# Staged first loads, other filler matmuls, and a planner that gives the shared port to whoever asked first: a two-layer hybrid trunk on one core

## The chip, the cores and the metric

The kernel runs on one core of one Trainium2 chip. The metric is the device time of one launch in microseconds (us), lower is better. Times of several runs are given by their median.

## The reference

A residual stream x of 512 tokens by 1024 channels passes two layers. In each layer a conditioning vector c gives shift, scale and gate; the normalized and modulated x is projected by one wide matrix, whose columns feed three causal token mixers (sparse attention over the top 128 keys, sliding-window attention with sinks, stick-breaking attention) and their gates; the merged result is projected back and added.

```python
for each layer:
    mod = silu(c) @ W_ada + b_ada             # shift, scale, gate
    u = rms_norm(x, g) * (1 + scale) + shift
    z = u @ W_in                              # all mixers, gates, merge gates
    y_b = mixer_b(z) * silu(gate_b)           # b = A, B, C
    merged = sum_b sigmoid(m_b) * (y_b @ W_br_b)
    x = x + gate * (merged @ W_out)
```

Everything is float32.

## The kernel before

**Matmuls.** x is held transposed, as 8 tiles of 128 channels by 512 tokens (k = 0 to 7; k = 0 to 3 in the tile `vc`, 4 to 7 in `va`). TensorE (PE) works on numbers rounded to a shorter form, so each weight chunk and each u is split into a high and a low part (`whi`, `wlo`, `uh`, `ul`), and each product is three matmuls: whi with uh, whi with ul, wlo with uh. A 256 KB chunk of weights is loaded into a tile `wstage` (four slots), cast to `whi`, and `wlo` is the difference of the two; the class `Chunks` (L632) loads and splits ahead of use.

**A recorded program.** No engine order is written by hand. The class `Recorder` (L244) notes every instruction with the engines that may run it, `price` (L304) gives it a modelled duration, and `forward` (L372) plans: it steps through the instructions, puts each at the earliest time that its engine, its inputs and its tile slots allow, and repeats this for five rounds, with the latest time that an instruction may start in one round (`latest`, L491) as its priority in the next. VectorE (DVE) and GpSimd (POOL) share a port in this model: of the instructions marked `port` only one runs at a time. For PE it also adds a cost when the shape of the matmul changes: modes are "c" (64 columns of the array, as in the mixers' products of probabilities and values), "t" (transposes) and "m" (all others). The best plan is emitted in order at L536, so every row of a profile has that line, and tiles are told apart by name. In the planner's loop the choice between engines is `if mine is not None and (best is None or mine < best[0])`, where `mine` is the triple of start time, priority and number: at equal start times the more urgent instruction goes.

**The start** (`start`, within `trunk`). Eight warm-up matmuls on ones, then silu(c) is broadcast over all partitions as `csr`. `norm(HALVES[0])` loads the first 256 tokens of x in four transfers, squares, sums and adds over partitions by a matmul with ones (`nones`), and makes 1/rms. `ada_load(j)` loads two tiles of 512 KB of the conditioning weights for channel tile j into slots called `Y` (five slots), and `ada_first(j)` (L706) makes shift and scale of that tile from each by one DVE scalar_tensor_tensor with csr, 128 by 1024, whose sum goes to `mods`, and `amul` from that. `make_u` (L755) turns x[k] into uh and ul by `mods` and `amul`. While PE has nothing to do, `ada_first` puts filler matmuls before the dot products: `FILL` (L42) says how many for each quarter of the weights, 11 in all, on the tiles `Y` as they land. `ch.load(1)` loads the two weight chunks of k = 0, `norm(HALVES[1])` the second half of x, and so on. All loads are issued by SyncE (SP) in one order and may start when their slot is free.

**What follows.** The first phase (`first_phase`, L893) takes seven output tiles over k = 0 to 7, k = 0 and 1 in halves of 256 tokens, then come the mixers, the merge gates and the output projection; the second layer repeats this without the start.

Of the kernel before, what the change touches and what calls it, by code (L numbers as in the profile page):

```python
# [32 lines left out]
S = 512  # L33
# [5 lines left out]
LOW = -3.0e38  # L39
TOPK = 128  # L40
WARM = 8
FILL = (2, 1, 4, 4, 0, 0, 0, 0)  # L42
BIG = 2.0 ** 100
SPACE = {"c0": 865, "c1": 7720, "c2": 1802, "a0": 1361, "a1": 13022, "a2": 500, "b0": 2448, "b1": 10119, "b2": 1676, "ag": 12129, "as": 6930, "t": 2422}
QCOST = 2408
# [198 lines left out]
class Recorder:  # L244
# [127 lines left out]
    def forward(self):  # L372
# [37 lines left out]
        while len(out) < len(self.list):  # L410
            best = None
            for name, e in E.items():
                free, pend, ready = e["free"], e["pend"], e["ready"]
                while pend and pend[0][0] <= free + 1e-9:
                    i = heapq.heappop(pend)[1]
                    ready[i] = self.list[i]
                mine = None
                for i in list(ready):
                    x = ready[i]
                    if x.taken:  # L420
                        del ready[i]
                        continue
                    y = x.alts[name]
                    at = max(free, port) if y.port else free
                    if len(x.alts) > 1 and self.elsewhere(x, name, at, E, port):
                        continue
                    key = (at, x.prio, i)
                    if mine is None or key < mine:
                        mine = key
                if mine is None or mine[0] > free + 1e-9:  # L430
                    while pend and self.list[pend[0][1]].taken:
                        heapq.heappop(pend)
                    if pend:
                        est, i = pend[0]
                        x = self.list[i]
                        at = max(est, port) if x.alts[name].port else est
                        key = (at, x.prio, i)
                        if (mine is None or key < mine) and not (len(x.alts) > 1 and self.elsewhere(x, name, at, E, port)):
                            mine = key
                        elif mine is None:  # L440
                            mine = None
                if mine is not None and (best is None or mine < best[0]):
                    best = (mine, name)
            assert best is not None, "no instruction may go"
            (at, _, i), name = best
            e, x = E[name], self.list[i]
            y = x.alts[name]
            x.taken, x.engine = True, name
# [1 line left out]
            hold = y.cost  # L450
            if name == "PE":
                if e["mode"] is not None and y.mode != e["mode"]:
                    hold += 0.18 if "c" in (y.mode, e["mode"]) else 0.08
                e["mode"] = y.mode
            x.start, x.hold = at, hold
            e["free"] = at + hold
# [102 lines left out]
def trunk(ctx, tc, xT, vecs, w_ss, w_gt, w_first, w_t, w_v, w_br, w_o, rope, consts, out):  # L559
# [68 lines left out]
    csr = fixed("csr", [P, D], F32)  # L628
    sk8 = fixed("sk8", [P, 8 * L], F32)


    class Chunks:  # L632
        LD, LS = LOAD_AHEAD, SPLIT_AHEAD
# [4 lines left out]
            self.used = set()  # L638
            self.nload = self.nsplit = 0

        def load(self, upto):
            while self.nload < min(upto + 1, len(self.seq)):
                i = self.nload
                if i >= 4 and i - 4 not in self.used:
                    break
                src, is_raw = self.seq[i][:2]
                n = src.shape[1]
                t = rec.tile("wstage", [P, S], F32)
                SP.dma_start(t[:, :n], src)
                self.raw[i] = (t, n)  # L650
                self.nload += 1
# [46 lines left out]
    def ada_ss(l, j, q):  # L698
        return op(0, lambda w: ada_step(l, j, q, w), (w_ss[l, j, q], True))

    def ada_load(j):
        st["wada", j] = [rec.tile("Y", [P, 2 * S], F32) for _ in range(2)]
        for i in range(2):
            SP.dma_start(st["wada", j][i].rearrange("p (a b) -> p a b", a=2), w_ss[0, j, 2 * i:2 * i + 2].rearrange("q p s -> p q s"))

    def ada_first(j):  # L706
        o = rec.tile("dot", [P, 4], F32)
        for i in range(2):
            w, m = st["wada", j][i], 8 * i + j
            if j < 2:  # L710
                for q in range(2):
                    for _ in range(FILL[4 * j + 2 * i + q]):
                        mm(st["nbank" if j else "warm"][:, :P], f(nones), w[:, S * q:S * q + P], not j)
            DVE.scalar_tensor_tensor(w, w, 1.0, csr, op0=OP.mult, op1=OP.mult, accum_out=o[:, i:i + 1])
            DVE.tensor_tensor(out=mods[0][:, m:m + 1], in0=o[:, i:i + 1], in1=b_ada[0][:, m:m + 1], op=OP.add)
        DVE.scalar_tensor_tensor(amul[0][:, j:j + 1], mods[0][:, 8 + j:9 + j], 1.0, g_sb[0][:, j:j + 1], op0=OP.add, op1=OP.mult)
# [665 lines left out]
    def start():  # L1382
# [17 lines left out]
        x = st["x"] = [xx[k // 4][:, k % 4] for k in range(KT)]  # L1400
        nb = st["nbank"] = st["rstd"] = sbank()

        def norm(cs_):
            for k in range(0, KT, 2):
                SP.dma_start(xx[k // 4][:, k % 4:k % 4 + 2, cs_], xT[:, k:k + 2, cs_])
            prev = None
            for k in range(0, KT, 2):
# [12 lines left out]
                prev = t  # L1420
            rstd_of(nb[:, cs_])

        norm(HALVES[0])
        for k in (0, 1):
            times_rstd(x[k], HALVES[0])
        ada_load(0)
        ada_first(0)
        ch.load(1)
        make_u(0, 0, x[0], HALVES[0])
        norm(HALVES[1])  # L1430
        for k in (0, 1):
            times_rstd(x[k], HALVES[1])
        ada_load(1)
        ada_first(1)
        make_u(0, 1, x[1], HALVES[0])
        make_u(0, 0, x[0], HALVES[1])
        make_u(0, 1, x[1], HALVES[1])
        ch.load(3)
        ada_load(2)

    sin_t = cos_t = tri0 = band = ident_b = cmask_b = None

# [110 lines left out]
```

## Time and profile before

| what | us |
|---|---|
| median of three runs | 1236.3 |
| the three runs | 1236.63, 1228.27, 1236.3 |
| the profiled execution | 1232.83 |
| its span in the trace | 1231.0 |
| PE busy in it | 1201.3 (98%) |
| DVE busy | 976.0 (79%) |
| ACT (ScalarE) busy | 559.5 (45%) |
| POOL busy | 258.2 (21%) |

The span runs from the first to the last instruction of the trace; the device time has 1.8 us around it. Busy time is what the engine spends in instructions other than waits and issues. In the profile PEld is the load of weights into the array, which runs beside the matmuls.

### The profile page before, as it was taken

How to read it: one execution, taken by the hardware profiler on the slowest of the kernel's cores; microseconds unless marked ns; L12 is line 12 of the kernel's file. 1: busy time of each engine (PE TensorE's matmuls, PEld its weight loads, DVE VectorE, ACT ScalarE, POOL GpSimd, SP SyncE). 2: the span in 40 equal slices, each digit the busy share in tenths (PEclk: the TensorE clock that was granted, in tenths of full speed). 3: DMA queues.
4: the chain of work that ended last, by engine and by line, in shares of the span. 5: the costliest groups of instructions: out<-in, count | busy, mean ns of one | idle time of the engine just before them, and what ended most of it. 6: DMA issues, size and time to landing. Idle time of an engine off the chain costs nothing.

```text
span 1231.0 us, 17835 instructions
## 1 busy us (share of the span) xinstructions
PE 1201.3 (98%) x5984; PEld 980.3 (80%) x5984; DVE 976.0 (79%) x2128; ACT 559.5 (45%) x1157; POOL 258.2 (21%) x278
## 2 busy tenths in 40 slices
PE   7999999999999999999999999999999999999997
PEld 6789777778878887778898987777787888877886
DVE  7966999999788887777475689999986888667654
ACT  4342678554256522642143258665533563244222
POOL 2210333433012211001211015253410111100120
PEclk8999999999999999999999999999999999999999
DMA  9644221324333455334533433223442333322343
GB/s 320 196 122 131 73 86 61 108 93 132 119 104 102 121 154 154 95 114 118 181 115 102 126 98 86 69 86 103 112 121 72 82 95 107 107 70 77 94 120 103
DMA packets 81915, 139.40 MB, mean 113 GB/s; under 512 B 10016, under 2 KB 22560, under 8 KB 81824
## 3 DMA queue, kind: packets, MB, share of 16 engines
q1 hardware_dynamic: 80672, 136.17, 37.8%
q10 hardware_dynamic: 1152, 2.10, 0.5%
q8 instruction: 47, 0.77, 0.3%
q14 instruction: 44, 0.36, 0.1%
HBM read 125.39 MB, written 4.19 MB: 105 GB/s over the span
## 4 chain that ended last, share of the span: by engine, by line
PE 79%; DVE 12%; ACT 3%; DMA 2%; issue 2%; SPq 1%; POOL 1%; DVEq 0%; ACTq 0%; POOLq 0%
PE ps_z L536 59%; PE ps_s L536 20%; DVE t L536 3%; ACT t L536 2%; DVE m L536 1%; DVE Q L536 1%; DVE score L536 1%; DMA wstage<-in_w_t 1%; DVE wstage L536 1%; SPq L536 1%; DVE Y L536 1%; DVE vc L536 1%; DVE e L536 1%; DMA vc<-in_xT 1%; DVE zc L536 0%
## 5 line engine op out<-in xcount | busy, mean ns | idle before, releaser
L536 PE MATMUL ps_z<-uh,whi 128*128 128x512 f32 (+1 forms) x908 | 357.8, 395 | 7.1 <-ACT uh L536 4.8
L536 PE MATMUL ps_z<-ul,whi 128*128 128x512 f32 (+1 forms) x908 | 356.8, 393 | 0.5 <-DVE ul L536 0.5
L536 PE MATMUL ps_z<-uh,wlo 128*128 128x512 f32 (+1 forms) x908 | 354.6, 391 | 0.9 <-DVE wlo L536 0.9
L536 POOL TENSOR_TENSOR wlo<-wstage,whi 128x512 fp32r<-128x512 f32 (+1 forms) x148 | 197.9, 1338 | 701.8 <-DVE whi L536 322.9
L536 PEld LDWEIGHTS ps_z<-uh,whi 128*128 128x128 f32 x908 | 170.3, 188 | 46.6 <-ACT uh L536 6.2
L536 PEld LDWEIGHTS ps_z<-ul,whi 128*128 128x128 f32 x908 | 171.0, 188 | 39.2 <-issue 3.3
L536 PEld LDWEIGHTS ps_z<-uh,wlo 128*128 128x128 f32 x908 | 170.5, 188 | 38.4 <-DVE wlo L536 1.6
L536 ACT CAST whi<-wstage 128x512 fp32r<-128x512 f32 (+2 forms) x153 | 90.8, 596 | 212.9 <-PE ps_z L536 147.5
L536 DVE CAST whi<-wstage 128x512 fp32r<-128x512 f32 (+2 forms) x169 | 69.8, 413 | 124.3 <-PE ps_z L536 104.9
L536 DVE TENSOR_TENSOR wlo<-wstage,whi 128x512 fp32r<-128x512 f32 (+2 forms) x224 | 147.3, 661 | 18.0 <-ACT whi L536 9.2
L536 PE MATMUL ps_z<-Y,whi 128*128 128x512 f32 x384 | 121.6, 396 | 0.2
L536 ACT ACTIVATE e<-ps_z 128x512 f32<-128x512 f32 x68 | 40.0, 592 | 121.7 <-PE ps_z L536 121.2
L536 PEld LDWEIGHTS ps_z<-Y,whi 128*128 128x128 f32 x384 | 71.6, 188 | 17.1 <-DVE xm L536 0.7
L536 ACT ACTIVATE e<-e 128x512 f32<-128x512 f32 x96 | 60.2, 631 | 40.4 <-DVE e L536 39.6
L536 PE MATMUL ps_z<-Y,wlo 128*128 128x512 f32 x192 | 76.0, 396 | 0.0
L536 ACT ACTIVATE t<-t 128x512 f32<-128x512 f32 x120 | 72.0, 627 | 5.5 <-DVE t L536 1.8
L536 ACT ACTIVATE t<-t,nm 128x256 f32<-128x256 f32 (+3 forms) x128 | 65.0, 510 | 18.5 <-DVE nm L536 18.5
L536 POOL CAST whi<-wstage 128x512 fp32r<-128x512 f32 (+1 forms) x50 | 31.4, 628 | 167.9 <-ACT vb L536 51.8
L536 PE MATMUL ps_s<-small,t 128*128 128x128 f32 x432 | 58.5, 275 | 4.6 <-ACT t L536 4.0
L536 PEld LDWEIGHTS ps_s<-small,t 128*128 128x128 f32 x432 | 49.7, 141 | 15.3 <-ACT t L536 7.3
L536 DVE SCALAR_TENSOR_TENSOR wstage<-wstage,csr 128x512 f32<-128x512 f32 x64 | 48.0, 751 | 10.6 <-DMA wstage<-in_w_ss 8.1
L536 DVE MAX8 m<-score 128x8 f32<-128x256 f32 (+2 forms) x96 | 53.3, 556 | 1.5
(201 smaller groups left out, 2080.3 us busy)
## 6 DMA issues: line engine op xcount, KB each, us to landing
wstage<-in_w_t SPq DMA_DIRECT2D x212, 256.0 KB, 2.7
wstage<-in_w_v SPq DMA_DIRECT2D x48, 182.0 KB, 2.4
Y<-in_w_ss SPq DMA_DIRECT2D x16, 512.0 KB, 6.4
m<-zs SPq DMA_DIRECT2D x128, 64.0 KB, 2.0
wstage<-in_w_gt SPq DMA_DIRECT2D x32, 256.0 KB, 2.6
wstage<-in_w_ss SPq DMA_DIRECT2D x32, 256.0 KB, 2.7
wstage<-in_w_o SPq DMA_DIRECT2D x32, 256.0 KB, 2.7
wstage<-in_w_first SPq DMA_DIRECT2D x16, 256.0 KB, 3.4
```

The lines of the kernel that those rows point to most:

```text
L536: getattr(self.real[engine], y.op)(*[real(a) for a in y.args], **{k: real(v) for k, v in y.kw.items()})
```

## The change

Three things are changed.

1. **Loads in stages.** `behind(t, v)` lets POOL copy one column of v into a tile t just before a load into t. The copy needs v's landing, and the load needs the copy, so the load is issued only after v has landed. It stands before the first two weight chunks (behind x's last piece of the first half), before the four pieces of x's second half (behind the first chunk), and before the conditioning weights of tiles 1 and 2 (behind the first and second chunk).
2. **Fillers.** The 11 matmuls on `Y` are gone; `busy` puts 24 in their place, 12 on the two first weight chunks and 12 on x[0] and x[1] after their scaling.
3. **The planner.** At equal start times the instruction goes that could have started first (`asked`: the later of its inputs' time and its engine's); priority decides only after that. A change of matmul shape is assumed to cost 0.095 us where the 64-column form is on either side (0.18 before), and nothing otherwise (0.08 before).

```diff
-FILL = (2, 1, 4, 4, 0, 0, 0, 0)
...
-                if mine is not None and (best is None or mine < best[0]):
-                    best = (mine, name)
+                if mine is not None:
+                    asked = max(free, self.list[mine[2]].est)
+                    if best is None or (mine[0], asked, mine) < best[:3]:
+                        best = (mine[0], asked, mine, name)
             assert best is not None, "no instruction may go"
-            (at, _, i), name = best
+            (at, _, i), name = best[2:]
...
-                    hold += 0.18 if "c" in (y.mode, e["mode"]) else 0.08
+                    hold += 0.095 if "c" in (y.mode, e["mode"]) else 0.0
...
+    def behind(t, v):
+
+        POOL.tensor_copy(out=t[:, 0:1], in_=v[:, 0:1])
+
...
-        def load(self, upto):
+        def load(self, upto, after=None):
...
                 t = rec.tile("wstage", [P, S], F32)
+                if after is not None:
+                    behind(t, after)
                 SP.dma_start(t[:, :n], src)
...
-            if j < 2:
-                for q in range(2):
-                    for _ in range(FILL[4 * j + 2 * i + q]):
-                        mm(st["nbank" if j else "warm"][:, :P], f(nones), w[:, S * q:S * q + P], not j)
             DVE.scalar_tensor_tensor(w, w, 1.0, csr, op0=OP.mult, op1=OP.mult, accum_out=o[:, i:i + 1])
...
+        def busy(n, v):
+            for _ in range(n):
+                mm(st["warm"][:, :P], f(nones), v[:, :P], True)
+
         norm(HALVES[0])
+        ada_load(0)
+        ch.load(1, x[6])
+        busy(6, ch.raw[0][0])
+        busy(6, ch.raw[1][0])
+        ada_first(0)
         for k in (0, 1):
             times_rstd(x[k], HALVES[0])
-        ada_load(0)
-        ada_first(0)
-        ch.load(1)
+            busy(6, x[k])
         make_u(0, 0, x[0], HALVES[0])
-        norm(HALVES[1])
+        norm(HALVES[1], ch.raw[0][0])
+        ada_load(1, ch.raw[0][0])
         for k in (0, 1):
             times_rstd(x[k], HALVES[1])
-        ada_load(1)
         ada_first(1)
...
         ch.load(3)
-        ada_load(2)
+        ada_load(2, ch.raw[1][0])
```

`norm` and `ada_load` take an `after` too and put `behind` before their loads in the same way.

**SP's order at the start.** `wstage` are weight chunks, `Y` conditioning weights, `vc` and `va` the halves of x; numbers tell tiles apart. Before, from the first Y on:

```order
L536 DMA Y_115<-in_w_ss 128x2x512
L536 DMA Y_118<-in_w_ss 128x2x512
L536 DMA wstage_122<-in_w_first 128x512
L536 DMA wstage_125<-in_w_first 128x384
L536 DMA Y_131<-in_w_ss 128x2x512
L536 DMA Y_136<-in_w_ss 128x2x512
L536 DMA wstage_140<-in_w_first 128x512
L536 DMA wstage_146<-in_w_first 128x384
L536 DMA vc_100<-in_xT 128x2x256
L536 DMA Y_151<-in_w_ss 128x2x512
L536 DMA va_108<-in_xT 128x2x256 x2
L536 DMA Y_179<-in_w_ss 128x2x512
```

The last piece of x's second half (vc_100) follows directly on these. Now, from the third Y-and-chunk pair on:

```order
L537 DMA wstage_122<-in_w_first 128x512
L537 DMA wstage_125<-in_w_first 128x384
L537 DMA wstage_145<-in_w_first 128x512
L537 DMA wstage_149<-in_w_first 128x384
L537 DMA vc_100<-in_xT 128x2x256
L537 DMA Y_184<-in_w_ss 128x2x512
L537 DMA va_108<-in_xT 128x2x256 x2
L537 DMA Y_182<-in_w_ss 128x2x512
L537 DMA Y_188<-in_w_ss 128x2x512
L537 DMA Y_195<-in_w_ss 128x2x512
L537 DMA Y_198<-in_w_ss 128x2x512
L537 DMA wstage_226<-in_w_first 128x512
```

Three more chunks and then the last piece of x's second half (vc_100) follow on these. The chunks of k = 0, gated behind x, are now wstage_145 and 149; those of k = 1 (122 and 125) are not gated and stand ahead of them. Y_182 and 188 belong to k = 1, Y_195 and 198 to k = 2, Y_184 to k = 3.

**DVE's order before u of k = 1.** uh1 is the high part of that u, `mods0` shift and scale, the rows with csr the dot products. Before:

```order
L536 SCALAR_TENSOR_TENSOR Y_136,dot_201<-Y_136,csr_70 128x1024
L536 TENSOR_TENSOR mods0_72<-dot_201,small_66 128x1
L536 TENSOR_TENSOR t_244<-t_244 128x256
L536 SCALAR_TENSOR_TENSOR amul0_74<-mods0_72,small_66 128x1
L536 SCALAR_TENSOR_TENSOR Y_151,dot_254<-Y_151,csr_70 128x1024
L536 TENSOR_TENSOR t_250<-t_250 128x256
L536 TENSOR_SCALAR uh1_261<-vc_100,amul0_74,mods0_72 128x256
```

Now:

```order
L537 SCALAR_TENSOR_TENSOR Y_182,dot_279<-Y_182,csr_70 128x1024
L537 TENSOR_TENSOR mods0_72<-dot_279,small_66 128x1
L537 SCALAR_TENSOR_TENSOR Y_188,dot_279<-Y_188,csr_70 128x1024
L537 TENSOR_TENSOR mods0_72<-dot_279,small_66 128x1
L537 SCALAR_TENSOR_TENSOR amul0_74<-mods0_72,small_66 128x1
L537 SCALAR_TENSOR_TENSOR Y_195,dot_293<-Y_195,csr_70 128x1024
L537 TENSOR_TENSOR mods0_72<-dot_293,small_66 128x1
L537 SCALAR_TENSOR_TENSOR Y_198,dot_293<-Y_198,csr_70 128x1024
L537 TENSOR_TENSOR mods0_72<-dot_293,small_66 128x1
L537 SCALAR_TENSOR_TENSOR amul0_74<-mods0_72,small_66 128x1
L537 SCALAR_TENSOR_TENSOR Y_184,dot_303<-Y_184,csr_70 128x1024
L537 TENSOR_SCALAR uh1_307<-vc_100,amul0_74,mods0_72 128x256
```

The dot products for k = 2 and the first of k = 3 now stand between those of k = 1 and its u.

**PE's order at mixer b of the first layer.** `t` are probabilities and `vb` values (64 columns of the array each), small,t are transposes, vc,Q the scores of another mixer. Before:

```order
L536 MATMUL ps_s<-t,vb 64x256 x3
L536 MATMUL ps_s<-t,vb 64x128
L536 MATMUL ps_s<-t,vb 64x256 x3
L536 MATMUL ps_s<-t,vb 64x128
L536 MATMUL ps_z<-ul_485,whi 128x512
```

Now:

```order
L537 MATMUL ps_s<-t,vb 64x256 x3
L537 MATMUL ps_s<-t,vb 64x128
L537 MATMUL ps_s<-vc,Q 128x256 x4
L537 MATMUL ps_z<-uh_211,whi 128x512
L537 MATMUL ps_z<-ul_224,whi 128x512
L537 MATMUL ps_s<-vc,Q 128x256
L537 MATMUL ps_s<-small,t 128x128 x7
L537 MATMUL ps_s<-vc,Q 128x256 x5
L537 MATMUL ps_s<-vc,Q 128x128 x2
L537 MATMUL ps_s<-t,vb 64x256 x3
L537 MATMUL ps_s<-t,vb 64x128
```

The two halves of the group, which stood together, are separated by 14 other rows' matmuls. Four of the eight groups of mixer b stand apart in this way, and two more of the groups of mixers a and c. Over the whole program 17 wlo subtractions move from POOL to DVE (10 of them into the two stretches in which DVE looks for the top 128 keys), and about a dozen whi casts from ACT to DVE.

## Rows read from the trace of the kernel before

**Rows 1.** The page, busy time of each engine (share of the span, instructions).

```profile
PE 1201.3 (98%) x5984; PEld 980.3 (80%) x5984; DVE 976.0 (79%) x2128; ACT 559.5 (45%) x1157; POOL 258.2 (21%) x278
```

**Rows 2.** Busy time by stretch: us and instructions, then TensorE's granted clock, DMA.

```profile
12.30:16.00 3.70, 0.02 (x1) 0.02 (x1) 3.63 (x9) 1.12 (x2) 0.71 (x1) 1.00 1.06 376
17.40:27.60 10.20, 7.85 (x30) 6.84 (x29) 8.25 (x21) 2.88 (x6) 1.74 (x1) 0.50 1.06 380
48.00:66.50 18.50, 16.71 (x71) 12.18 (x69) 16.57 (x34) 8.07 (x14) 3.76 (x5) 1.00 0.45 151
...
200.00:300.00 100.00, 95.42 (x465) 74.58 (x464) 95.34 (x218) 55.27 (x121) 40.69 (x40) 1.00 0.36 106
...
800.00:900.00 100.00, 95.78 (x465) 75.99 (x465) 95.47 (x219) 55.86 (x122) 41.56 (x41) 1.00 0.36 103
```

**Rows 3.** Timeline of ACT at the start: start, duration, what, [idle before <- releaser].

```profile
7.29 0.63 ACT L536 ACTIVATE t<-va 128x512 f32<-128x512 f32 x1 [0.57 <-DMA va<-in_xT]
...
11.39 0.51 ACT L536 CAST whi<-wstage 128x384 fp32r<-128x384 f32 x1 [0.28 <-DMA wstage<-in_w_first]
...
21.03 0.63 ACT L536 ACTIVATE t<-vc 128x512 f32<-128x512 f32 x1 [1.49 <-DMA vc<-in_xT]
```

**Rows 4.** Timeline of PE at the start (each 128-column filler counts as two).

```profile
10.21 2.05 PE L536 MATMUL ps_s<-Y,nones 128*128 128x128 f32 x16
15.98 0.50 PE L536 MATMUL ps_z<-uh,whi 128*128 128x256 f32 x2 [3.71 <-ACT uh L536]
...
16.79 0.28 PE L536 MATMUL ps_z<-uh,whi 128*128 128x256 f32 x1
16.91 0.28 PE L536 MATMUL ps_z<-ul,whi 128*128 128x256 f32 x1
...
21.42 0.79 PE L536 MATMUL ps_z<-uh,whi 128*128 128x256 f32 x2 [2.35 <-DVE uh L536]
```

**Rows 5.** The page, DMA issues: instructions, KB each, us from issue to landing.

```profile
wstage<-in_w_t SPq DMA_DIRECT2D x212, 256.0 KB, 2.7
```

**Rows 6.** Timeline of DVE and POOL, two dot products and the wlo beside one.

```profile
29.84 1.22 DVE L536 SCALAR_TENSOR_TENSOR Y<-Y,csr 128x1024 f32<-128x1024 f32 x1
...
31.60 1.31 POOL L536 TENSOR_TENSOR wlo<-wstage,whi 128x512 fp32r<-128x512 f32 x1 [12.46 <-PE ps_z L536]
...
31.66 2.33 DVE L536 SCALAR_TENSOR_TENSOR Y<-Y,csr 128x1024 f32<-128x1024 f32 x1
```

**Rows 7.** Timeline of PE, the first phase's last matmul.

```profile
65.32 0.39 PE L536 MATMUL ps_z<-uh,wlo 128*128 128x512 f32 x1
```

**Rows 8.** Timeline of PE, groups of mixer b, and the matmul behind one.

```profile
250.59 2.65 PE L536 MATMUL ps_s<-t,vb 128*64 128x256 f32 x16
253.16 0.50 PE L536 MATMUL ps_z<-ul,whi 128*128 128x512 f32 x1
...
345.99 0.65 PE L536 MATMUL ps_s<-t,vb 128*64 128x256 f32 x2
348.04 2.25 PE L536 MATMUL ps_s<-t,vb 128*64 128x256 f32 x14
...
370.16 2.25 PE L536 MATMUL ps_s<-t,vb 128*64 128x256 f32 x16
...
943.54 1.73 PE L536 MATMUL ps_s<-t,vb 128*64 128x256 f32 x8
```

**Rows 9.** The page, costliest groups: busy, mean ns, idle before, releaser.

```profile
L536 POOL TENSOR_TENSOR wlo<-wstage,whi 128x512 fp32r<-128x512 f32 (+1 forms) x148 | 197.9, 1338 | 701.8 <-DVE whi L536 322.9
...
L536 DVE TENSOR_TENSOR wlo<-wstage,whi 128x512 fp32r<-128x512 f32 (+2 forms) x224 | 147.3, 661 | 18.0 <-ACT whi L536 9.2
```

**Rows 10.** PE's waits from 100 to 1231 us: total, times, longest.

```profile
PE ps_s L536 <- ACT t L536: 4.0, 3, 2.0
PE ps_s L536 <- DVE Q L536: 3.4, 2, 1.7
...
PE ps_z L536 <- DVE wlo L536: 0.9, 2, 0.5
```

More of the change, by code (lines that the diff above doesn't have):

```diff
@@ L699, in ada_ss, with ada_load @@
         return op(0, lambda w: ada_step(l, j, q, w), (w_ss[l, j, q], True))
-    def ada_load(j):
+    def ada_load(j, after=None):
         st["wada", j] = [rec.tile("Y", [P, 2 * S], F32) for _ in range(2)]
         for i in range(2):
+            if after is not None:
+                behind(st["wada", j][i], after)
             SP.dma_start(st["wada", j][i].rearrange("p (a b) -> p a b", a=2), w_ss[0, j, 2 * i:2 * i + 2].rearrange("q p s -> p q s"))
@@ L1401, in start, with norm @@
         nb = st["nbank"] = st["rstd"] = sbank()
-        def norm(cs_):
+        def norm(cs_, after=None):
             for k in range(0, KT, 2):
+                if after is not None:
+                    behind(xx[k // 4][:, k % 4, cs_], after)
                 SP.dma_start(xx[k // 4][:, k % 4:k % 4 + 2, cs_], xT[:, k:k + 2, cs_])
```

## The prediction

> **What bounds the kernel now.** I read the shares first: TensorE (PE) is busy for 1201.3 us of a span of 1231.0, so whatever changes the time has to change PE's busy time or the 30 us in which it idles [rows 1]. The table by stage says where these lie. From 200 to 300 us PE loses 4.6 us while VectorE (DVE) works 95%; 800 to 900 us is the same stage of the second layer and loses 4.2 [rows 2]. The largest part is the start: nothing runs on PE between 12.3 and 16.0 us, and after that gap the granted clock is 0.50 (1.2 GHz, against 1.00 before and later) for 10.2 us, in which PE is busy for 7.85 [rows 2]. The last view is the timeline of the start. x's first half is there at 7.3 us and the first split weights at 11.4 [rows 3]. PE bridges part of the wait with fillers until 12.3, then idles 3.71 us until the first u exists, and 2.35 us before k=1 because DVE has not made uh1 [rows 4]. x's second half lands last at 21.0 us [rows 3].
>
> **The start, step by step.** The transfers come first. A gated load is issued only after the landing that it waits for. The chunks for k=0 now stand behind k=1's (the first ungated pair), so 448 KB more come ahead of them. By the rate of 376 GB/s [rows 2] that is 1.2 us over the 11.4 of before for the pair, 0.7 for its first part: about 12.1 us. Only then does the next transfer start, on an empty queue. A load of 256 KB takes 2.7 us from issue to landing [rows 5] and 0.7 us at the full rate, so the gap costs 2.0 us. Ahead of x's last piece of the second half stand one 512 KB Y and four chunks (896 KB) more than before: 1.4 MB at 380 GB/s is 3.7 us. It lands at 21.0 + 2.0 + 3.7 = 26.7 us, the Y before these chunks 2.4 us and one x piece (0.7 us) earlier, at 23.6.
>
> PE next. The 24 fillers replace 11. Eight of the old ones took 2.05 us at full clock [rows 4], 0.256 each, so 24 take 6.1 us, from 12.1 to 18.2. They stand ahead of the first real matmul in PE's order, which started at 15.98: 2.2 us later. The 10 added copies of one column lie on POOL, which has nothing to do there until its first wlo, and hold back only loads, not DVE or PE; at worst each waits for one dot product on DVE, 1.2 us, which comes out of the same gap in the transfers. The first half of k=0 is 21 matmuls at steps of 0.117 us (16.79 to 16.91 [rows 4]), 2.5 us, to 20.7.
>
> Then comes the step that I think decides. On DVE, uh1 stood behind the dot products of Y_131, Y_136 and Y_151. Now it stands behind those of Y_182, Y_188, Y_195, Y_198 and Y_184. The load of Y_198 lands at 23.6; two dot products of 1.22 us [rows 6], their small rows and uh1 itself (0.4) add 3.0: uh1 is there at 26.6. PE idles from 20.7 to 26.6, 5.9 us, in place of 3.71 + 2.35.
>
> From 21.42, where uh1 let PE go on before, to the end of the first phase at 65.71 [rows 4, 7] it took 44.3 us. Of these, about 1.6 were idle time late in the phase (from 48 to 66.5 PE is busy for 16.71 of 18.5 us [rows 2], 0.2 of the rest behind the last matmul) and about 3.1 the half clock (half of the 6.2 us that ran from 21.42 to 27.6). I let the late waits go, since PE comes later to each u now. 39.6 us remain at full clock, from 26.6, so the phase ends at 66.2: +0.5. But the one idle time of this length in the trace (3.71 us) was followed by a stretch at 1.2 GHz in which 7.85 us of work ran, half of it lost: 3.9 us. A gap of 5.9 us that starts after only 8 us of work is more likely than not to bring it again. Start: **+0.5 to +4.4; I take +4.4**, by the nearest row. Below nothing it can go to -6.3 + 2.2 = -4.1, if uh1 is not late and the clock stays.
>
> **The planner, part 1: matmuls of 64 columns.** They pass the array in pairs, two halves at a time. The 16 matmuls of one block pair of mixer b take 2.65 us where the halves follow each other, 2.25 where they overlap in part, and two separate groups of 8 take 1.73 each (one of two such rows is shown), 3.46 together [rows 8]. In the new order four of the eight such groups are pulled apart: two of the 2.65 kind (+0.81 each), one of 2.25 (+1.21) and one that stood as 0.65 + 2.25 (+0.56): **+3.4**. The plan does this because it now believes that a change of matmul shape costs 0.095 us and not 0.18. In mixers a and c two more groups are pulled apart; at the price of b's that is 1.7 us, and nothing if their halves still overlap: I take **+0.8**. All of it is on PE, which is the bound, and nothing hides it.
>
> The Trainium skill bears on this: TensorEngine Tiling (Array Packing), Key Properties, says that a change of tiling mode drains TensorE. If a drain cost a whole matmul of 0.39 us, seven more groups (14 changes) would cost 5.5 us. The rows of before agree only weakly: the matmul behind a group is 0.50 us long and not 0.39 [rows 8], 0.11 per change, which is the planner's new figure and lies within the durations used above. The sum goes without this.
>
> **The planner, part 2: the port and the waits in the body.** Of the wlo subtractions 17 move from POOL to DVE, and a dozen casts from ACT to DVE. A wlo takes 0.66 us on DVE and 1.34 on POOL [rows 9]. Ten of the 17 fall into the two stretches where DVE is at 95% [rows 2]: 10 x 0.66 = +6.6 us at worst, for all 17 +11.2. Outside these two stretches DVE is busy for (976.0 - 190.8) of 1031 us, 76% [rows 1, 2], and they cost nothing. On the other side stand the waits that PE has there for DVE and ACT: 4.0 + 3.4 + 0.9 = 8.3 us in six or seven pieces [rows 10]. A plan whose costs are nearer to the chip could lose them; so -8.3 to +11.2. I take nothing, as the two bounds are about equally far and these waits are for long chains (Q, t) and not for the port.
>
> Sum: +4.4 + 3.4 + 0.8 + 0 = +8.6 us on the profiled execution of 1232.83 us (span 1231.0 and 1.8 around it): **1241.4 us**. That execution lies 3.5 us under the median of the three runs, 1236.3, which lie 8.4 apart; so against the median I forecast +5.1, or 0.4%, which a measurement here (about 1%, 12.4 us) would call no change.
>
> **The rivals.**
> (1) The clock stays. PE works without a break up to 20.7, and a busier beginning may carry it over the gap: the granted clock stayed 1.00 through the gaps of 1.7 to 2.0 us between 200 and 300 us [rows 2, 10]. Against: 5.9 us is three times as long. 1241.4 - 3.9 = 1237.5.
> (2) The plan fits the chip. The first asked, first served rule and the cheaper shape changes make the plan's times true, and PE's waits in the body go: 1241.4 - 8.3 = 1233.1, with the clock kept 1229.2. For: a dot product of 1.22 us took 2.33 beside a wlo of 1.31 on POOL [rows 6], so one of the two does wait for the other's whole length, and the old plan let the more urgent one pass first. The page SBUF - State Buffer of the Trainium skill, section on the two separate sides, says the same: the port is an exclusive lock for whichever starts first. It gives no further price. Against: of the 8.3 us, 7.4 are named for t and Q, long chains, and 0.9 for wlo.
> (3) The change does what it says: fillers bridge, k=1 is not late, no half clock. -4.1 + 4.2 = +0.1: 1232.9. Against: the order of DVE and SP, which puts x's second half and uh1 later.
> (4) Slower by over 1%: DVE becomes the bound of the top-k stretches. Of 100 us it has 4.7 free there; once the added wlo and casts use these up, each 0.66 us more is 0.66 us on PE: 1241.4 + 6.6 = 1248.0, for all 17 1252.6. For: ten of the moved wlo fall there. Against: a POOL that runs fewer of them holds DVE up less (1.1 us at each meeting [rows 6]).
>
> **How the numbers follow.** The forecast (half clock, groups apart, body unchanged) 0.42; (1) 0.18; (2) 0.18; (3) 0.07; (4) 0.15. The forecast's own range is 1237 to 1246: the median's 3.5 us up, the a and c groups at -0.8 and +0.9, the clock's stretch shorter. The range of 8 in 10 reaches down into (2), 1226, and up to (4) with all 17, 1253. Faster by over 1% (below 1223.9) needs (2) with the clock kept and a term that I do not know: 0.09. Slower by over 1% (above 1248.7) is most of (4) and the upper edge of the forecast: 0.16. Within 1%: 0.75.
>
> **What would show it.** In the profile after: 24 fillers from about 12.1 to 18.2; the first real matmul at 18.2; uh1's matmul at about 26.6 with an idle time of some 6 us named for DVE uh; clock 0.50 for about 10 us behind it (the step that I am least sure of); the last matmul of the first phase near 70 us, 66 with the clock kept; halves of mixer b as groups of 8 at 1.73 us; PE's waits from 200 to 300 us still near 4.6. The forecast is wrong if the first phase ends before 65 us, if the b groups overlap although they stand apart in the order, or if PE loses under 1 or over 8 us in 200 to 300.

## The result and the profile after

The changed kernel takes 1244.91 us (median of 7 runs, 1243.53 to 1248.61), the kernel before 1236.63 (7 runs, 1228.27 to 1238.3): a ratio of 1.0079, 95% interval 1.0063 to 1.0095. It is slower by 0.8%, within the 1% that the prediction called no change, and inside its range. The profiled execution is 1244.91 us with a span of 1243.1, 12.1 more than before.

The page of the changed kernel, busy time of each engine, as [rows 1]:

```profile
PE 1213.1 (98%) x6010; PEld 987.0 (79%) x6010; DVE 964.4 (78%) x2128; ACT 556.7 (45%) x1154; POOL 250.4 (20%) x291
```

PE is busy for 11.8 us more and the span is 12.1 longer: nearly all of the loss is work of PE that takes longer, not waiting. DVE is busy for 11.6 us less with the same number of instructions. In the trace 19 wlo and 15 casts of whi have come to it (224 to 243 and 169 to 184; the text ahead of the prediction says 17 and a dozen), and as many others have left it. By their kinds, some 9.5 us of the fall are instructions that take less time than before. That POOL holds them up less often fits this; no run isolates it.

Timeline of PE, as [rows 4, 7]. The last row is the first 128x364 matmul, which opens the stage behind the first phase:

```profile
13.12 4.88 PE L537 MATMUL ps_s<-wstage,nones 128*128 128x128 f32 x24 [2.79 <-DMA wstage<-in_w_first]
17.83 2.84 PE L537 MATMUL ps_s<-vc,nones 128*128 128x128 f32 x24
20.43 0.36 PE L537 MATMUL ps_z<-uh,whi 128*128 128x256 f32 x1
...
29.91 0.80 PE L537 MATMUL ps_z<-uh,whi 128*128 128x256 f32 x2 [6.72 <-DVE uh L537]
...
72.16 0.40 PE L537 MATMUL ps_s<-whi,uh 128*128 128x364 f32 x1 [0.22 <-DVE zc L537]
```

The same matmul before:

```profile
66.88 0.41 PE L536 MATMUL ps_s<-whi,uh 128*128 128x364 f32 x1 [0.63 <-DVE zc L536]
```

So in these two traces the start has cost 5.3 us (72.16 against 66.88), and the rest of the program, the body, from there to the end of the span, 6.8 us (1170.9 against 1164.1).

Timeline of ACT and DVE at the start, as [rows 3, 6]: the last piece of x's second half, the dot products of k = 2 and 3, and uh1 behind them.

```profile
26.76 1.23 DVE L537 SCALAR_TENSOR_TENSOR Y<-Y,csr 128x1024 f32<-128x1024 f32 x1 [0.90 <-DMA Y<-in_w_ss]
...
28.30 1.22 DVE L537 SCALAR_TENSOR_TENSOR Y<-Y,csr 128x1024 f32<-128x1024 f32 x1
...
29.44 0.41 DVE L537 TENSOR_SCALAR uh<-vc,amul,mods 128x256 fp32r<-128x256 f32 x1
```
```profile
29.77 0.63 ACT L537 ACTIVATE t<-vc 128x512 f32<-128x512 f32 x1 [9.41 <-DMA vc<-in_xT]
```

uh1 is made when the second dot product behind Y_198's landing ends, as the prediction said, but that landing came at 26.7 and not at 23.6.

Busy time by stretch, as [rows 2] (us and instructions of PE, PEld, DVE, ACT, POOL; granted clock; DMA share, GB/s):

```profile
10.30:13.10 2.80, 0.03 (x1) 0.01 (x1) 2.70 (x8) 1.62 (x4) 0.00 (x0) 0.52 0.41 155
13.10:17.20 4.10, 4.08 (x19) 4.10 (x20) 3.19 (x8) 2.79 (x6) 1.54 (x8) 0.50 0.63 182
17.20:22.90 5.70, 5.70 (x51) 5.70 (x51) 2.53 (x7) 1.26 (x2) 0.00 (x0) 1.00 1.02 380
22.90:29.90 7.00, 0.28 (x3) 0.08 (x1) 5.93 (x16) 0.13 (x1) 0.00 (x0) 0.83 1.06 381
29.90:34.30 4.40, 4.39 (x14) 3.86 (x15) 3.71 (x10) 0.50 (x1) 0.00 (x0) 0.50 1.03 371
...
200.00:300.00 100.00, 96.66 (x475) 75.04 (x474) 92.93 (x215) 56.98 (x125) 39.11 (x41) 1.00 0.35 98
800.00:900.00 100.00, 97.37 (x472) 75.70 (x470) 90.87 (x211) 56.28 (x125) 40.27 (x45) 0.98 0.32 95
846.70:850.10 3.40, 3.40 (x14) 3.01 (x13) 3.40 (x21) 0.00 (x0) 0.49 (x1) 0.50 0.21 77
```

The half clock stands where it was expected, behind the idle 6.72 us, and also before it: it stood at 0.52 while PE idled from 10.3 to 13.1 us, and the fillers themselves ran at 1.2 GHz up to 17.2. In the body PE loses 3.3 and 2.6 us in the two top-k stages, where it lost 4.6 and 4.2.

Groups of mixer b, as [rows 8]:

```profile
255.73 1.73 PE L537 MATMUL ps_s<-t,vb 128*64 128x256 f32 x8
260.32 1.73 PE L537 MATMUL ps_s<-t,vb 128*64 128x256 f32 x8
...
350.40 0.65 PE L537 MATMUL ps_s<-t,vb 128*64 128x256 f32 x2
351.89 1.29 PE L537 MATMUL ps_s<-t,vb 128*64 128x256 f32 x6
353.54 1.73 PE L537 MATMUL ps_s<-t,vb 128*64 128x256 f32 x8
```

Then something that no view before had shown me. Both traces hold a stretch of 72 matmuls of 128x512 one behind the other, without a wait. First and 72nd of them, before:

```profile
425.67 0.48 PE L536 MATMUL ps_z<-uh,whi 128*128 128x512 f32 x1
...
442.08 0.40 PE L536 MATMUL ps_z<-uh,wlo 128*128 128x512 f32 x1
```

and after:

```profile
433.21 0.48 PE L537 MATMUL ps_z<-uh,whi 128*128 128x512 f32 x1
...
449.84 0.40 PE L537 MATMUL ps_z<-uh,wlo 128*128 128x512 f32 x1
```

That is 16.41 / 71 = 231.1 ns from one to the next before, and 16.63 / 71 = 234.2 ns after, at a granted clock of 1.00 in both. Over all uninterrupted 128x512 matmuls behind the first phase (3,407 and 3,391 pairs in the two traces) the mean step is 231.17 and 232.53 ns. 1.36 ns times 3,400 is 4.6 us, which is two thirds of the body's loss and stood nowhere in the prediction.

### The profile page after: what moved, and what is told of

It reads as the page before. It is cut to its first block, busy times and chain, and to the rows that moved or that the text cites. A ratio compares the mean times of both kernels' runs of the same rounds, so it can differ in the third digit from the quotient of the medians.

```text
span 1243.1 us, 17931 instructions
## 1 busy us (share of the span) xinstructions
PE 1213.1 (98%) x6010; PEld 987.0 (79%) x6010; DVE 964.4 (78%) x2128; ACT 556.7 (45%) x1154; POOL 250.4 (20%) x291
## 4 chain that ended last, share of the span: by engine, by line
PE 86%; DVE 7%; DMA 2%; ACT 2%; SPq 1%; issue 1%; POOL 0%; DVEq 0%; ACTq 0%; POOLq 0%
PE ps_z L537 64%; PE ps_s L537 22%; SPq L537 1%; DVE t L537 1%; DVE Q L537 1%; ACT t L537 1%; DMA Y<-in_w_ss 1%; DVE zc L537 1%; DVE m L537 1%; DMA m<-zs 1%; DVE vc L537 1%; DVE wlo L537 0%; DVE wstage L537 0%; DMA wstage<-in_w_first 0%; DMA va<-in_xT 0%
## 5 line engine op out<-in xcount | busy, mean ns | idle before, releaser
L537 PE MATMUL ps_z<-uh,whi 128*128 128x512 f32 (+1 forms) x908 | 361.5, 399 | 7.8 <-DVE uh L537 6.7
L537 POOL TENSOR_TENSOR wlo<-wstage,whi 128x512 fp32r<-128x512 f32 (+1 forms) x129 | 171.5, 1330 | 652.6 <-DVE whi L537 326.9
L537 DVE CAST whi<-wstage 128x512 fp32r<-128x512 f32 (+2 forms) x184 | 76.5, 416 | 131.6 <-PE ps_z L537 111.9
L537 DVE TENSOR_TENSOR wlo<-wstage,whi 128x512 fp32r<-128x512 f32 (+2 forms) x243 | 158.2, 655 | 12.6 <-ACT whi L537 3.9
L537 ACT CAST whi<-wstage 128x512 fp32r<-128x512 f32 (+2 forms) x140 | 82.9, 594 | 182.6 <-PE ps_z L537 121.7
```

Of the source, the lines that this page charges most:

```text
L537: getattr(self.real[engine], y.op)(*[real(a) for a in y.args], **{k: real(v) for k, v in y.kw.items()})
```

## The experiments

Each of the 12 kernels ran beside the kernel before on the same chip; ratios are to it. Two theories opened the study. One: the late start and the separated groups make the loss, and the step of the matmuls is an accident of one execution. The other: the step belongs to the changed kernel.

**The kernel before once more**, unchanged.

> The kernel before once more, for a second trace of it. The 512-column matmuls step by 0.231 to 0.233 us in the first trace of before and by 0.234 in that of after, which over some 3,600 of them is 4 us. Theory (the first trace of before is a quick execution, the step belongs to the execution and not to the kernel): this trace shows 0.233 to 0.234 and a body (from the first 364-column matmul to PE's end) of 1158 to 1161 us against 1156.9, and the time is near the median 1236.6. Rival (the order of the kernel after makes the step longer): again 0.231 to 0.232 and 1156.9.

One run, 1232.38 us. The step is 231.15 ns over 3,402 pairs and the body (to the end of PE) is 1155.7 us against 1156.9: the rival is right. The step belongs to the kernel, and a second trace of the same kernel repeats it to 0.02 ns.

The second trace also shows what does not repeat. Its first 364-column matmul, its longest wait in the second top-k stage, and the stretch behind that wait:

```profile
67.65 0.40 PE L536 MATMUL ps_s<-whi,uh 128*128 128x364 f32 x1 [0.63 <-DVE zc L536]
...
834.72 2.69 PE L536 MATMUL ps_s<-vc,Q 128*128 128x256 f32 x16 [2.06 <-DVE Q L536]
...
836.00:839.40 3.40, 3.40 (x13) 2.96 (x13) 3.40 (x22) 0.81 (x2) 2.29 (x3) 0.51 0.07 25
```

The start ends 0.8 us later than in the first trace, PE loses 3.3 and 3.1 us in the two top-k stages in place of 4.6 and 4.2, its waits behind 100 us are 7.7 us in place of 10.3, and the clock falls once where it had not. Differences of this size between two kernels are not shown by one trace of each.

**The new start alone.** The planner's lines are those of before:

```diff
-                if mine is not None:
-                    asked = max(free, self.list[mine[2]].est)
-                    if best is None or (mine[0], asked, mine) < best[:3]:
-                        best = (mine[0], asked, mine, name)
+                if mine is not None and (best is None or mine < best[0]):
+                    best = (mine, name)
...
-                    hold += 0.095 if "c" in (y.mode, e["mode"]) else 0.0
+                    hold += 0.18 if "c" in (y.mode, e["mode"]) else 0.08
```

> The new start (gates and fillers) with the old planner; in its order the body has the same 32 groups of 64-column matmuls as before. Theory (the start costs 5.3 us by itself: uh1 at 29.9 us behind five dot products, then half the clock): the first 364-column matmul at 72 us against 66.9, PE's waits after it as before (12 us), time 1236.6 + 5.3 = 1242. Rival (the start is caught up later, or the planner's numbers make all of the loss): 1237.

1243.26 us, ratio 1.0066 (1.0051 to 1.0081): +8.1 us, as much as nearly the whole change. PE at uh1, and its first 364-column matmul:

```profile
28.56 0.80 PE L535 MATMUL ps_z<-uh,whi 128*128 128x256 f32 x2 [6.29 <-DVE uh L535]
...
70.86 0.41 PE L535 MATMUL ps_s<-whi,uh 128*128 128x364 f32 x1 [0.22 <-DVE zc L535]
```

That matmul is 4.0 us later than before (3.2 against the second trace), so half of the loss or more lies behind the start, in a body whose order is nearly that of before. Its mean step is 232.57 ns. The new start makes the whole program's matmuls slower.

The tie rule needs no run: with it undone in the kernel after, or in the new start with the old costs, the planner puts out the same order on all five engines, row for row; put into the kernel before it moves one row on PE and one on DVE. What the planner's change does is done by the two costs of a change of shape.

**The new costs alone.** Old start, old tie rule:

```diff
-                    hold += 0.18 if "c" in (y.mode, e["mode"]) else 0.08
+                    hold += 0.095 if "c" in (y.mode, e["mode"]) else 0.0
```

> The old start with the new costs of a change of shape and the old tie rule; the order shows 39 groups of 64-column matmuls and 15 pieces of mixer b, as in the kernel after. Theory: b's pieces +3.4 us, groups of a and c -2.1, PE's waits in the body -2.4, more changes of shape about +2 and the step of the matmuls as in before: 1236.6 + 1 to 3 = 1238 to 1240, with the start as before (first 364-column matmul near 66.9). Rival (the plan fits the chip better, waits go and the loss of the kernel after is all start): 1234. Second rival (the new order also slows each matmul): 1241.

1236.50 us, ratio 1.0015 (1.0000 to 1.0030), 1.3 us over the kernel before beside it and within the 1 to 3 that the theory had. The separated groups cost what they gain elsewhere but for some 2 us. The step is 231.19 ns, that of the kernel before: the many moved matmuls don't change it.

**A bridge over the gap.** 32 more fillers in the kernel after:

```diff
+        busy(32, f(st["ul"][0]))
         norm(HALVES[1], ch.raw[0][0])
```

> The kernel after with 32 more filler matmuls on u's low part of k = 0, ahead of k = 0's first half in PE's order; nothing else in any order moves. Theory (the half clock behind uh1 comes from the idle 6.7 us before it): uh1 still at 29.9 us, granted clock 1.00 from there on, 4.4 us of work at half speed gone: first 364-column matmul at 70.0 in place of 72.2, time 1244.9 - 2.2 = 1242.7. Rival (the clock falls for another reason, or DVE and the loads are next in line): clock 0.50 again, or 72 us all the same, 1244.9.

1243.15 us, ratio 1.0067 (1.0052 to 1.0082) against 1.0079 of the kernel after. The stretches in front of and behind uh1, and PE there:

```profile
17.00:30.00 13.00, 13.00 (x117) 13.00 (x116) 9.44 (x24) 1.90 (x3) 0.00 (x0) 1.00 1.03 375
28.80:34.00 5.20, 4.92 (x36) 4.51 (x34) 4.52 (x13) 1.38 (x5) 0.00 (x0) 1.00 1.05 386
```
```profile
19.71 7.31 PE L537 MATMUL ps_s<-ul,nones 128*128 128x128 f32 x64
...
29.37 0.40 PE L537 MATMUL ps_z<-uh,whi 128*128 128x256 f32 x2
...
69.43 0.40 PE L537 MATMUL ps_s<-whi,uh 128*128 128x364 f32 x1 [0.22 <-DVE zc L537]
```

With PE busy up to uh1 the clock stays at 1.00; the five traces with the new start and no bridge (the kernel after, the new start alone, and three kernels below) all have a stretch at 0.50 around uh1. It is shown that the idle time brings the half clock. What it is worth has to be counted from uh1 on, since the loads before it come earlier or later from one execution to the next (without a bridge the stage behind the first phase begins at 69.5 us in one trace of this order and at 72.2 in another). From uh1's matmul to the first 364-column one it took 40.1 us here and 41.4 to 42.3 in the five, so the half clock was worth 1.3 to 2.2 us; 2.2 were expected from 4.4 us of work at half speed. The intervals of the two ratios overlap, so the medians do not show the gain.

**Where tiles lie.** The new start changes which tile is first used when, and tiles get their addresses in that order. A tile `dot` of 16 bytes in each partition takes 32 and falls between the large ones, in another place with each start. The offsets modulo 64 bytes at which tiles begin, read from the two built programs:

```
            whi (4 slots)   wlo (4 slots)   uh0, ul0   uh1 .. uh7, ul1 .. ul7
before      0  0 32 32      0 32 32 32      32         32
after       0  0  0  0      0  0  0  0       0         32
```

The new start alone has the offsets of after, the new costs alone those of before: just as the steps are divided. Each 128x512 matmul of the traces, put together with the addresses of its moving tile (mostly u) and its weights (stationary), gives the mean step by the distance of the two, modulo 64:

```
            distance 0          distance 32
before      229.8 ns (1,974)    233.1 ns (1,384)
after       229.8 ns   (614)    233.2 ns (2,604)
```

That is a correlation. The next two kernels change one size, so that the offsets agree and no instruction moves:

```diff
-        o = rec.tile("dot", [P, 4], F32)
+        o = rec.tile("dot", [P, 16], F32)
```

(and the same at the second place where `dot` is made).

> The kernel before with one size changed: the tile `dot` has 64 bytes in each partition in place of 16, so that all large tiles allocated behind it, whi and wlo, uh and ul, begin at the same offset modulo 64 bytes. In the kernel before half of the weight tiles begin 32 bytes off the u tiles, in the kernel after nearly all. Theory (a 512-column matmul steps by 229.4 ns where moving and stationary tile share the offset and by 233.3 where not; the new start changes the order in which tiles get their addresses, and that makes the body of the kernel after 4 to 5 us longer): the mean step goes from 231.15 to 229.4 ns, 3,400 x 1.75 = -6.0 us, time 1235.2 - 6.0 = 1229.2. Rival (the step follows from the order of work or from the execution): 231.1 again and 1235.

1229.84 us, ratio 0.9965 (0.9952 to 0.9978), step 229.8 ns. The kernel before gains 3.5 us (1233.3 beside it) from 48 unused bytes in each of two slots; 6.0 were expected.

> The kernel after with the same one size changed. Theory: the mean step goes from 232.5 to 229.4 ns, 3,400 x 3.1 = -10.5 us, time 1244.9 - 10.5 = 1234.4, 5 us over the aligned kernel before in place of 8 to 10: what is left are the start (first 364-column matmul at 71 to 72 us against 67) and the groups of 64 columns. Rival: 232.5 and 1244.9, or the same distance of 9 us to the aligned kernel before.

1242.44 us, ratio 1.0067 (1.0042 to 1.0092): the expectation missed by 8 us. The step fell only to 230.9 ns, worth 5.6 us, and the body of this trace shows nothing of it (1164.3 us against 1163.7 in the kernel after). The waits of PE behind 100 us are 10.3 us against 8.5, and two stretches at half clock, where the kernel after has one, cost 1.7 more; the other 2.7 us have no name. Such waits and stretches differ between two traces of one kernel too, so the miss is explained in part at most:

```profile
243.50:246.90 3.40, 3.40 (x13) 2.92 (x12) 3.40 (x20) 0.00 (x0) 0.25 (x1) 0.50 0.31 81
281.00:284.40 3.40, 3.40 (x10) 2.62 (x9) 2.80 (x8) 2.41 (x6) 1.54 (x2) 0.50 0.44 149
```

PE at uh1, and the first 364-column matmul; the order is that of the kernel after, where these rows stand at 29.91 and 72.16:

```profile
27.57 0.80 PE L537 MATMUL ps_z<-uh,whi 128*128 128x256 f32 x2 [4.48 <-DVE uh L537]
...
69.47 0.40 PE L537 MATMUL ps_s<-whi,uh 128*128 128x364 f32 x1 [0.25 <-DVE zc L537]
```

The 64-byte rule was too coarse. With all distances 0 modulo 64, those modulo 512 still told steps apart in the aligned kernel before: 228.2 ns at 0, 230.0 at 64, 232.0 at 384, 233.3 at 448. In the aligned kernel after most distances are 64, but there the pairs at distance 0 step by 230.7 ns as well, so the distance of the two tiles alone does not give the step.

**Fillers alone and gates alone**, with the old planner and `dot` at 64 bytes.

Fillers alone, against the new start:

```diff
-        ch.load(1, x[6])
+        ch.load(1)
...
-        norm(HALVES[1], ch.raw[0][0])
-        ada_load(1, ch.raw[0][0])
+        norm(HALVES[1])
+        ada_load(1)
...
-        ada_load(2, ch.raw[1][0])
+        ada_load(2)
```

> Old planner, aligned tiles, the 24 new fillers without the gates: loads are issued as in the kernel before. Theory (the gates make the loads late, the fillers are harmless and can even keep the clock): the fillers run from 11 to about 16.6 us without an idle time over 1 us before, the clock stays 1.00 up to uh1 at about 21.5, first 364-column matmul at 64 to 65.5 us, time 1229.2 - 2 = 1227. Rival (the fillers delay the start, or DVE is next in line and takes the gain): first 364-column matmul at 67 or later, 1229 to 1231.

1232.81 us, ratio 0.9994 (0.9977 to 1.0011). PE at u of k=1, and the first 364-column matmul:

```profile
26.75 0.38 PE L535 MATMUL ps_z<-uh,whi 128*128 128x256 f32 x1 [2.46 <-ACT uh L535]
...
67.42 0.40 PE L535 MATMUL ps_s<-whi,uh 128*128 128x364 f32 x1 [0.28 <-DVE zc L535]
```

The rival as to the start, though the time is above its 1229 to 1231: the fillers bring nothing and cost nothing, and the start ends at a time that the order of before takes as well (66.9 to 68.0 us in five traces). They did not keep the clock either: PE idled 2.26 us before them, and the first of them ran at 1.2 GHz, up to 17.2 us.

Gates alone, against the new start:

```diff
-        busy(6, ch.raw[0][0])
-        busy(6, ch.raw[1][0])
...
-            busy(6, x[k])
```

> Old planner, aligned tiles, the gates without any fillers. Theory: the loads behind the gates land as in the kernel after, uh1 at 27 to 30 us, half the clock behind the idle time, first 364-column matmul at 70 to 72 us, time 1229.2 + 4.5 = 1233.7. Rival (the 24 fillers in front of the first matmul make the start late): first 364-column matmul at 67, 1229.

1232.89 us, ratio 1.0000 (0.9985 to 1.0014). The same two rows:

```profile
23.24 0.50 PE L535 MATMUL ps_z<-uh,whi 128*128 128x256 f32 x2 [2.03 <-ACT uh L535]
...
67.08 0.40 PE L535 MATMUL ps_s<-whi,uh 128*128 128x364 f32 x1 [0.62 <-DVE zc L535]
```

My theory missed here: the gates alone don't delay the start either. In this plan both pieces of x's second half that lie in `vc` are issued first behind the gate, and ACT makes uh1 by 23.2. Only fillers and gates together gave the order in which x's last piece stands behind five Y and four chunks, and uh1 behind five dot products. How the planner comes to that order I have not traced. The medians of these two kernels can't price gates and fillers, since their steps (230.4 and 230.9 ns) differ again from the 229.8 of the aligned kernel before; the first phase can.

**All large tiles at one offset.** `dot` at 512 bytes in each partition (`[P, 128]`), in three kernels.

> The kernel before with `dot` at 512 bytes in each partition (64 in the aligned kernels): now u, weights, Y, Q and x tiles all begin at the same offset modulo 512. With 64 bytes some pairs of moving and stationary tile still stood 64, 384 or 448 bytes apart (modulo 512), and their 512-column matmuls stepped by 230 to 233 ns where those at distance 0 stepped by 228.2. Theory (the step follows the distance of the two tiles' offsets): mean step 228.3 ns against 229.8, 3,400 x 1.5 = -5 us against the aligned kernel before at 1229.8: 1225. Rival (only the 64-byte offset counts, or what PE gains turns into waits): 1229 to 1230.

1225.91 us, ratio 0.9926 (0.9912 to 0.9939), mean step 227.5 ns. The 72 matmuls of above:

```profile
422.89 0.48 PE L536 MATMUL ps_z<-uh,whi 128*128 128x512 f32 x1
...
439.10 0.39 PE L536 MATMUL ps_z<-uh,wlo 128*128 128x512 f32 x1
```

16.21 / 71 = 228.3 ns. This is the fastest kernel of the study and beats both.

> The kernel after with `dot` at 512 bytes, so that both kernels have the same offsets and the same step, 228.3 ns. Theory (of the 8 to 10 us between the two kernels the start's late loads are 3 to 5, the costs of shapes 2, and the rest came from the addresses): 4 to 7 us over the kernel before of the same layout, 1229 to 1232. Rival (addresses play no part in the difference between the two): 9 to 10 us over it, 1235.

1232.48 us, ratio 0.9994 (0.9979 to 1.0009), mean step 227.6 ns, as in the kernel above. At equal offsets the change costs 1232.48 - 1225.91 = 6.6 us. PE at uh1 and behind the first phase:

```profile
28.81 0.80 PE L537 MATMUL ps_z<-uh,whi 128*128 128x256 f32 x2 [5.41 <-DVE uh L537]
...
70.75 0.40 PE L537 MATMUL ps_s<-whi,uh 128*128 128x364 f32 x1 [0.26 <-DVE zc L537]
```

> Only the new start, with the old planner, with `dot` at 512 bytes. Theory: step 228.3 ns, first 364-column matmul at 69 to 72 us, time 3 to 5 us over the kernel before of the same layout: 1228 to 1230. Rival: 8 us over it as without the layout, 1233.

1229.54 us, ratio 0.9957 (0.9943 to 0.9970): the start alone costs 3.6 us at equal offsets, and the new costs on top of it 2.9. Without the layout the start alone cost 8.1, so some 4.5 of these were offsets.

**All weights off by 32 bytes.** The order of before, `dot` at 512 bytes, and 32 unused bytes before and behind each slot of whi and wlo:

```diff
-        return self.pool.tile(list(shape), dtype, name=self.name, tag=f"{self.name}_{slot}", bufs=1)
+        off = self.name in ("whi", "wlo") and slot not in self.seen
+        self.seen.add(slot)
+        if off:
+            self.pool.tile([P, 8], F32, name="pad", tag=f"pad_{self.name}_{slot}", bufs=1)
+        t = self.pool.tile(list(shape), dtype, name=self.name, tag=f"{self.name}_{slot}", bufs=1)
+        if off:
+            self.pool.tile([P, 8], F32, name="pad", tag=f"pad2_{self.name}_{slot}", bufs=1)
+        return t
```

> The kernel before with `dot` at 512 bytes and 32 unused bytes before and behind each of the eight slots of whi and wlo, so that every weight tile begins 32 bytes (modulo 64) off every u tile; the order of work is that of the kernel before on every engine. Theory: all 512-column matmuls of u step by 233.3 ns, mean 233.3 against 231.15 in the kernel before and 228.3 in the one with one offset for all: 1234 + 3,400 x 2.15 = 1241, 16 us over the latter. Rival (the step doesn't follow from the tiles' offsets): 1225 to 1234.

1240.54 us, ratio 1.0046 (1.0032 to 1.0061), mean step 232.5 ns. The same 72 matmuls:

```profile
429.49 0.47 PE L543 MATMUL ps_z<-uh,whi 128*128 128x512 f32 x1
...
446.04 0.39 PE L543 MATMUL ps_z<-uh,wlo 128*128 128x512 f32 x1
```

16.55 / 71 = 233.1 ns. The same instructions in the same order take 14.6 us more than at equal offsets, 1240.54 against 1225.91. That the place of u and weights sets the step is shown; by which distance, modulo what, is a reading that fits these kernels and not the aligned kernel after.

| kernel, order of before | offsets of u and weights | mean step, ns | us |
|---|---|---|---|
| `dot` at 512 bytes | all equal modulo 512 | 227.5 | 1225.9 |
| `dot` at 64 bytes | all equal modulo 64 | 229.8 | 1229.8 |
| before | mixed | 231.2 | 1233 to 1237 |
| weights moved by 32 bytes | all 32 apart modulo 64 | 232.5 | 1240.5 |

## Why the prediction was right, and where it was not

The time (1241.4 forecast, 1244.9 measured) and the sign came out, and the deciding step of the start is in the trace as described. The sum of +8.6 us also meets the medians (+8.3); 1241.4 lies lower because it starts from a quick execution of the kernel before. But terms were missing or wrong in opposite directions, so the sum is better than its parts.

- **uh1 behind five dot products: right, and later than I had.** 29.9 us measured, 26.6 forecast; 27.6 and 28.8 in the two other traces of this order (`dot` at 64 and at 512 bytes), so it is late by 1.0 to 3.3 us, changing with the execution. The gate opened at 13.1, not 12.1, and the gap in the transfers, 2.0 us in the sum, was larger: from 10.3 to 17.2 us they ran at 155 and 182 GB/s in place of 380, which loses 3.8 us. x's last piece came 8.7 us later than before (29.8 against 21.0), not 5.7. The idle time was 6.72 us for 5.9.
- **Fillers to 18.2 us: wrong in size.** They took up to 20.4, because the clock fell in the idle 2.8 us before them and stayed at half up to 17.2. It cost nothing, since uh1 came much later; with fillers alone the start ends at 67.4.
- **Half clock behind the gap, +3.9: right in kind, too large.** 4.4 us of work ran at half speed; the bridge gave back 1.3 to 2.2. I had taken the whole stretch of before, but here part of it fell on the idle time. Start in all +5.3 in the first two traces for +4.4 forecast; at equal offsets, 70.75 against 67.09, +3.7; over five traces of each start, 70.7 against 67.4 on average, +3.3. So the late uh1 was priced too low and the half clock too high.
- **Groups of mixer b, +3.4: right.** By the rows: two groups of 1.73 for one of 2.65 (+0.81, in either layer), 3.67 for 2.90 (+0.77), and the group that was one of 2.25 now as 0.65 + 1.30 + 1.73 (+1.43): +3.8. Each row overlaps the next a little; from the start of each group to the start of the matmul behind it, the sum rose from 18.9 to 22.4 us, +3.4. That the matmul behind a group takes 0.50 us and not 0.39 is not the price of the changed shape alone: one behind full-width transposes takes 0.48 (at 249.63 in the trace before).
- **Groups of mixers a and c, +0.8: wrong sign.** Counted in the same way, their sum fell by 2.2 us, from 48.0 to 45.8. Of these 0.8 are two waits within groups of before; the other 1.4 are work: other groups now overlap their halves.
- **Waits in the body, 0: right, as far as the traces tell.** All waits of PE behind 100 us come to 8.5 us against 10.3 before:

```profile
PE ps_s L537 <- DVE Q L537: 2.0, 3, 0.9
PE ps_s L537 <- DVE t L537: 1.5, 3, 0.9
PE ps_s L537 <- ACT t L537: 1.3, 4, 0.5
```

  The waits for t from ACT fell from 4.0 to 1.3, those for Q from 3.4 to 2.0, and new short ones (zc, vc, xm) take their place. But the sum of all waits is 7.7 to 10.5 us in five traces of the order of before, and 8.5, 10.3 and 11.8 in three of the order of after: no gain is shown, and with it nothing of rival (2).
- **Rival (4), DVE at its bound: did not come.** In the two stages DVE went from 95% to 93% and 91%. DVE's total is 973 to 976 us in five traces of the order of before and 964 to 966 in three of the order of after. Part of it is other work that left DVE; the larger part, shorter instructions, fits the argument against this rival, that DVE no longer waits for POOL's wlo. The Trainium skill's page SBUF - State Buffer, section SBUF: two separate sides, has the port as a lock for whichever starts first; the fall of DVE's busy time by 11.6 us, with 19 fewer wlo on POOL, agrees with it.
- **Rival (2)'s reason, the tie rule: wrong.** The rule moves nothing; what the plan gained came from the costs of shape.
- **What no step named: the step of the matmuls.** I priced PE's unmoved work at nothing. It grew by 1.36 ns in each 128x512 matmul, 4.6 us, because the start moved a 32-byte tile. Between the first two traces the waits are 1.8 us less, 0.8 of it counted in a and c above, and the half clock from 846.7 to 850.1 cost 1.7; both belong to the execution. The body's sum is 4.6 + 3.4 - 2.2 - 1.0 + 1.7 = 6.5 of 6.8 us.

The chance of 0.42 for the forecast's case and the bound of 1253 served well; the lucky part is that the missing +4.6 was met by 3.0 too much for a and c and by a start that on average costs 1.1 less than forecast.

## What to carry to other kernels

When a change touches which tiles exist or when they are first used, compare the step of an untouched stretch of back-to-back matmuls, in two traces of each kernel, before looking for causes in the order: a difference of 1% there is worth more than most waits. Keep small tiles from falling between large ones (round them up, or place them at the end), so that moving and stationary tiles share an offset. And a gate on a load moves all that is queued behind it: read from the planned order whether what is needed first is also issued first.

## What I had not expected of the hardware

A 128x512 matmul (fp32r) follows the last one after 227.5 ns on average where the moving tile and the weights begin at the same offset modulo 512 bytes (1225.9 us in all), and after 232.5 ns on average where all weights stand 32 bytes (modulo 64) off (1240.5 us), at a granted clock of 1.00 in both stretches of 72. The cause inside the chip stays open: whether it is the read of the moving tile, the load of the next weights beside it, or both, no run tells apart. Also, the granted clock fell to 0.50 for a short stretch in the top-k stages of most traces: in the kernel after behind three idle times of 0.3 to 0.9 us (from 846.7 on), in the aligned kernel after at 243.5 and 281.0. It comes and goes with the execution: in the first trace of the kernel before single waits of 1.7 to 2.0 us in the same stages [rows 10] were not followed by a fall, and in its second trace one of 2.06 us was (from 836.0 on), as was one of 1.99 us in the kernel before with `dot` at 512 bytes (from 237.6 on). What decides it is not settled by these runs.
